# The output projection of a hybrid attention step by seven block products per group of tokens, with the sums of weight blocks kept in DRAM

## The chip, the cores and the metric

One core of one Trainium2 chip runs the kernel. The metric is device microseconds for one execution; the figure for a kernel is the median of its runs.

## The reference

One layer of an encoder. 1024 new frames of a prompt and 8 x 16 new frames of running streams (the "sample") are normalised and projected with one weight matrix into queries, keys, values and gates of two groups of eight heads: stick-breaking attention and retention. Each head's output is normalised and gated, and all are put beside each other as `y`. The part that this case is about comes last:

```python
def merge(o_sb, o_r, gate_sb, gate_r, g_sb, g_r, w_out):
    y_sb = head_rms_norm(o_sb, g_sb, gate_sb.dtype) * jax.nn.silu(gate_sb)
    y_r = head_rms_norm(o_r, g_r, gate_r.dtype) * jax.nn.silu(gate_r)
    y = jnp.concatenate([y_sb, y_r], axis=-1)
    return jnp.einsum('bte,ed->btd', y, w_out)      # y: 1024 + 128 rows of 2048; w_out: 2048 x 2048
...
xp = xp + rms_norm(out, norm_post[l])               # rms_norm(x, g) = x * rsqrt(mean(x*x) + EPS) * g
xs = xs + rms_norm(out, norm_post[l])
```

Everything is float32.

## The kernel before

Tokens come in tiles of 128 rows: eight of the prompt (0 to 7) and the sample tile. They form two groups: tiles 0 to 3 with the sample, and tiles 4 to 7. For each group in turn the kernel projects head by head with weights streamed from DRAM (`project`, `project_rows`, L248 and L268) and weaves the attention and retention of the head before into it. What a head gives goes to DRAM as `s_y[group][head]`, with 128 features on the partitions and the tokens along the row.

Matrix products are made from halves. `split` (L135) takes a float32 tile and makes a rounded high part on ScalarE (L136) and the rest as a low part on VectorE (L137); three matmuls (high x high, high x low, low x high) give the product. A weight tile is loaded by the SP queue into `wr`, then split into `wh` and `wl`; the pool `wp` has four buffers of each.

The order of the woven work is set by a clock of ticks. The code that emits matmuls calls `tick()` (L180) after every few of them; a `Job` is a generator that yields after how many ticks it wants its next step, and each tick runs one step of one job that is due. `drain(job)` ticks without matmuls until a job is done. Each engine and each queue runs its instructions in the order in which they were emitted.

The output projection (`out_panel`, L1048, and `out_project`, L1101) takes the nine tiles in three chunks of three. For a chunk it runs over four panels of 512 columns of `w_out`, and in each over 16 blocks of 128 rows: one weight tile is loaded and split and used by three tiles, nine matmuls (L1066 to L1068). `load_moving` (L203) loads and splits the rows of `y` of the next chunk meanwhile, as a job. Behind each panel `take` (L1115) squares the accumulator for the norm on ScalarE (L1117) and multiplies it by the gain on VectorE (L1118); after the last panel `store` (L1125) scales, adds the residual row `xr` on VectorE (L1131) or GpSimd (L1129) and sends the row out. For the last chunk the last 256 columns of the weights are kept on chip (`keep_last`, L1090), so that each tile can be finished by itself at the end (L1173 to L1175).

In the second group of tokens GpSimd has the masks of attention (L511) and issues the transfers that turn the attention rows through DRAM (L479, L486).

Of the kernel before, what the change touches and what calls it, by code (L numbers as in the profile page):

```python
# [9 lines left out]
F32 = mybir.dt.float32  # L10
# [6 lines left out]
P = 128  # L17
D = 2048
# [32 lines left out]
D_KL = 29  # L51
# [5 lines left out]
D_TK = 4  # L57
D_FIN = 4
D_MR = 6
EPS = 1e-6  # L60
# [5 lines left out]
def tile_hybrid_step(  # L66
# [62 lines left out]
    s_S = [scr.tile([P, P], F32, name=f"s_S{h}") for h in range(H)]  # L129
    s_y = [  # L130
# [72 lines left out]
    def load_moving(mov, at, n, src, stage=None):  # L203
        hi, lo = mov
        for k in range(KT):
            q, j = divmod(k, WQ)
            if q == len(hi):
                for x, y in zip(mov, moving_part(mp, NMAX, q)):
                    x.append(y)
            pool, bufs = stage or (wp, 2)  # L210
            r = pool.tile([P, n], F32, name="mr", tag="mr", bufs=bufs)
            nc.sync.dma_start(r, src(k))
            split(hi[q][:, j, at : at + n], lo[q][:, j, at : at + n], r)
            yield D_MR

# [38 lines left out]
    def project_pair(g, mov, cols, loads=None):  # L254
# [3 lines left out]
        for w in range(KT // WQ):  # L258
            for i, (acc, chunk) in enumerate(zip(accs, chunks)):
                _, wh, wl = next(chunk)  # L260
                for _ in range(WQ if loads and w and i == 0 else 0):
                    next(loads)
# [5 lines left out]
    def project_rows(g, mov, col, dst, off, loads=None):  # L268
# [5 lines left out]
        for w in range(KT // 2):  # L274
# [5 lines left out]
            for _ in range(WQ if loads and w == 0 else 0):  # L280
                next(loads)
# [25 lines left out]
    with ExitStack() as s1:  # L307
# [621 lines left out]
        from_y = lambda k: s_y[0][k][:, : 3 * P]  # L929
        ret_job = sb_job = sub = loads = after = None  # L930
        for gi, g in enumerate(GROUPS):
# [7 lines left out]
            for h in range(H):  # L939
# [28 lines left out]
                def attention():  # L968
# [4 lines left out]
                    if gi == 1 and h == 0:  # L973
# [3 lines left out]
                        ip = s1.enter_context(tc.tile_pool(name="ip2", bufs=1))  # L977
                    q2 = [kq.tile([P, NB_TOK], F32R, name=f"q{c}", tag=f"q{c}") for c in "hl"]
# [31 lines left out]
                def gates():  # L1010
# [6 lines left out]
                    loads = load_moving(after, 0, *((NB_TOK, from_h), (3 * P, from_y, (ip, 6)))[gi])  # L1017
# [19 lines left out]
        main = after  # L1037

        def part(gi, tiles, mov, at):
            return [(t, gi, mov, at + i * P) for i, t in enumerate(tiles)]  # L1040

        def fetch(chunk):
            _, gi, mov, at = chunk[0]
            n = len(chunk) * P
            lo = GROUPS[gi]["tiles"].index(chunk[0][0]) * P
            yield from load_moving(mov, at, n, lambda k: s_y[gi][k][:, lo : lo + n])

        def out_panel(chunk, p, pools, ticks, loads=None, between=None, width=512):  # L1048
            pool = pools[p % len(pools)]
            cols = slice(p * 512, p * 512 + width)  # L1050
            acc = [pool.tile([P, 512], F32, name="a3", tag=f"acc{n % 2}") for n in range(len(chunk))]
            for k in range(KT):
                if loads and k < WQ:
                    next(loads)
                wr = wp.tile([P, width], F32, name="wr3", tag="wr")
                load = nc.sync.dma_start(wr, w_out[0, k * P : (k + 1) * P, cols])
                if between and k % 6 == 5:
                    with tc.issue_after(load.ins):
                        next(between, None)
                wh = wp.tile([P, width], F32R, name="wh3", tag="wh")  # L1060
                wl = wp.tile([P, width], F32R, name="wl3", tag="wl")
                split(wh, wl, wr)
                q, j = divmod(k, WQ)
                for a, (_, _, (hi, lo), at) in zip(acc, chunk):
                    ts = slice(at, at + P)
                    nc.tensor.matmul(a[:, :width], hi[q][:, j, ts], wh, start=(k == 0), stop=False)  # L1066
                    nc.tensor.matmul(a[:, :width], hi[q][:, j, ts], wl, start=False, stop=False)  # L1067
                    nc.tensor.matmul(a[:, :width], lo[q][:, j, ts], wh, start=False, stop=(k == KT - 1))  # L1068
                    for _ in range(ticks):
                        tick()  # L1070
            return acc

        chunk1 = part(0, (0, 1, 2), main, 0)
        panel0 = out_panel(chunk1, 0, (accp,), D_OUT, loads)
# [3 lines left out]
    with ExitStack() as s3:  # L1078
        c3 = s3.enter_context(tc.tile_pool(name="c3", bufs=1))
        rp = s3.enter_context(tc.tile_pool(name="rp", bufs=1))  # L1080
        accq = s3.enter_context(tc.tile_pool(name="accq", bufs=2, space=PSUM))
# [6 lines left out]
        LAST = slice(7 * 256, 8 * 256)  # L1088

        def keep_last(at):  # L1090

            hi, lo = main
            for q in range(KT // WQ):
                for j in range(0, WQ, 2):
                    wr = wp.tile([P, 2, 256], F32, name="wr4", tag="wr")
                    k = (q * WQ + j) * P
                    nc.sync.dma_start(wr, w_out[0, k : k + 2 * P, LAST].rearrange("(k p) e -> p k e", p=P))
                    split(hi[q][:, j : j + 2, at : at + 256], lo[q][:, j : j + 2, at : at + 256], wr)
                    yield D_KL

        def out_project(chunk, panel0=None, kept=None):  # L1101
            m = len(chunk)
            parts = 4 if kept is None else 5
            outs = [rp.tile([P, D], F32, name="out", tag="out", bufs=5) for _ in chunk]
            ssq = rp.tile([P, m, 5], F32, name="ssq3", tag="ssq3", bufs=2)
            xrs = []

            def load_x_rows():
                for t, _, _, _ in chunk:
                    xr = rp.tile([P, D], F32, name="xr", tag="xr", bufs=3)  # L1110
# [157 lines left out]
```

## Time and profile before

| | |
|---|---|
| runs | 2385.1, 2389.83, 2397.73 us; median 2389.83 |
| profiled execution | 2393.5 us, of which the span of instructions is 2391.8 us |
| TensorE busy in the span | 2320.5 us (97%) |
| VectorE, ScalarE, GpSimd busy | 1255.6, 920.0 and 644.1 us |
| granted TensorE clock | 0.991 of full |
| moved by transfers | 418.68 MB, mean 175 GB/s |

Busy time counts the instructions of an engine; those that only issue a transfer or wait are left out on the other engines, while GpSimd's own transfers count as its work. A row of a group reads: line, engine, operation, out<-in, shapes, count | busy us, mean ns of one | idle us just before them, and what ended that idle time. In a row of the timeline stand the start, the length and the instruction. PE is TensorE, DVE VectorE, ACT ScalarE, POOL GpSimd, SP the queue that issues most loads.

### The profile page before, as it was taken

Reading aid. Unit: us, or ns where it says so; the run is one execution under the profiler, and the core shown is the slowest. Engines: PE = TensorE matmul, PEld = TensorE weight load, DVE = VectorE, ACT = ScalarE, POOL = GpSimd, SP = SyncE. Lnnn points to the kernel's source line nnn. Section 1 sums busy time; section 2 is a strip of 40 time slices with the busy share of each in tenths; the row PEclk is TensorE's granted clock in tenths of the full one; section 3 lists DMA queues with packets and bytes.
Section 4 is the critical chain, followed back from the end, with each engine's and each line's share of the span. In section 5 each row is a group of like instructions: output and inputs, shape, how many; then the busy total and the mean of one; then the engine's idle time right before and its main releaser. Section 6 shows DMA issues by size and latency. Waiting matters only on the chain.

```text
span 2391.8 us, 40520 instructions
## 1 busy us (share of the span) xinstructions
PE 2320.5 (97%) x14832; PEld 2092.4 (87%) x14832; DVE 1255.6 (52%) x2442; ACT 920.0 (38%) x1937; POOL 644.1 (27%) x1033
## 2 busy tenths in 40 slices
PE   7999999999999999999899999999999999999998
PEld 7998899998999999998778989889898888888887
DVE  7245545455545555456545554554554566564544
ACT  6323333333333333334333334333343444443443
POOL 3144354434445353434202112020220220000000
PEclk9999999999999999999999999999999999999999
DMA  7659779796989979698866565555655666765563
GB/s 245 163 131 215 161 162 200 163 200 153 199 177 200 188 163 205 158 207 221 187 182 154 139 149 154 139 145 151 150 154 134 161 160 197 229 211 182 188 192 131
DMA packets 677049, 418.68 MB, mean 175 GB/s; under 512 B 224752, under 2 KB 620016, under 8 KB 674544
## 3 DMA queue, kind: packets, MB, share of 16 engines
q1 hardware_dynamic: 524272, 285.99, 48.0%
q0 software_dynamic: 32256, 71.36, 13.9%
q10 hardware_dynamic: 120320, 58.74, 9.1%
q8 instruction: 116, 1.90, 0.4%
q14 instruction: 85, 0.70, 0.1%
HBM read 336.24 MB, written 79.69 MB: 174 GB/s over the span
## 4 chain that ended last, share of the span: by engine, by line
PE 71%; DMA 6%; DVE 4%; issue 2%; ACT 2%; SPq 1%; POOL 0%; DVEq 0%; ACTq 0%; POOLq 0%
PE acc L234 36%; PE accn L293 12%; PE a L1067 5%; PE a L1066 5%; PE a L1068 5%; PE pa L623 2%; PE z L593 2%; DMA wr<-w_in 2%; PE zc L672 1%; PE pd L741 1%; DMA mr<-s_y 1%; DMA mr<-s_h 1%; DMA dT<-c_dt 1%; DVE wl L137 1%; PE pa L786 1%
## 5 line engine op out<-in xcount | busy, mean ns | idle before, releaser
L234 PE MATMUL acc<-mh,wh 128*128 128x256 f32 (+2 forms) x2304 | 667.2, 341 | 7.8 <-ACT wh L136 7.2
L137 DVE TENSOR_TENSOR wl<-wr,wh 128x512 fp32r<-128x512 f32 (+1 forms) x576 | 391.4, 684 | 517.7 <-ACT wh L136 500.8
L234 PE MATMUL acc<-ml,wh 128*128 128x256 f32 (+2 forms) x2304 | 661.5, 339 | 0.0
L234 PE MATMUL acc<-mh,wl 128*128 128x256 f32 (+2 forms) x2304 | 660.8, 339 | 0.0
L136 ACT ACTIVATE wh<-wr 128x512 fp32r<-128x512 f32 (+1 forms) x576 | 358.0, 625 | 726.6 <-PE acc L234 229.7
L234 PEld LDWEIGHTS acc<-mh,wh 128*128 128x128 f32 x2304 | 421.2, 189 | 40.5 <-ACT wh L136 9.0
L234 PEld LDWEIGHTS acc<-mh,wl 128*128 128x128 f32 x2304 | 424.5, 189 | 31.7 <-issue 2.5
L234 PEld LDWEIGHTS acc<-ml,wh 128*128 128x128 f32 x2304 | 425.5, 189 | 28.6 <-issue 0.8
L656 POOL DMA_DIRECT2D kc<-cache_sb_k x512 | 332.5, 655 | 344.4 <-DVE kcT L696 209.5
L293 PE MATMUL accn<-whn,mh 128*128 128x256 f32 x1152 | 329.2, 287 | 4.6 <-DVE rg L320 4.5
L293 PE MATMUL accn<-wln,mh 128*128 128x256 f32 x1152 | 326.3, 284 | 2.4 <-DVE wln L137 2.4
L293 PE MATMUL accn<-whn,ml 128*128 128x256 f32 x1152 | 325.9, 284 | 0.0
L293 PEld LDWEIGHTS accn<-whn,mh 128*128 128x128 f32 x1152 | 220.9, 192 | 8.5 <-DVE rg L320 4.8
L293 PEld LDWEIGHTS accn<-wln,mh 128*128 128x128 f32 x1152 | 221.7, 192 | 3.4 <-DVE wln L137 2.6
L293 PEld LDWEIGHTS accn<-whn,ml 128*128 128x128 f32 x1152 | 221.3, 192 | 0.0
L1067 PE MATMUL a<-wl,mh 128*128 128x512 f32 (+1 forms) x576 | 219.4, 381 | 1.1 <-DVE wl L137 1.1
L1066 PE MATMUL a<-wh,mh 128*128 128x512 f32 (+1 forms) x576 | 218.9, 381 | 0.1
L1068 PE MATMUL a<-wh,ml 128*128 128x512 f32 (+1 forms) x576 | 218.9, 380 | 0.0
L137 DVE TENSOR_TENSOR wln<-wrn,whn 128x512 fp32r<-128x512 f32 x128 | 87.3, 689 | 125.1 <-ACT whn L136 124.8
L136 ACT ACTIVATE whn<-wrn 128x512 fp32r<-128x512 f32 x128 | 79.6, 632 | 164.7 <-PE acc L234 70.7
L486 POOL DMA_DIRECT2D be<-s_be x128 | 94.3, 743 | 132.4 <-DMA s_be<-be 114.5
L1067 PEld LDWEIGHTS a<-wl,mh 128*128 128x128 f32 x576 | 108.3, 188 | 22.4 <-DVE wl L137 2.2
(195 smaller groups left out, 2617.6 us busy)
## 6 DMA issues: line engine op xcount, KB each, us to landing
wr<-w_in SPq DMA_DIRECT2D x384, 256.0 KB, 4.2
wr<-w_out SPq DMA_DIRECT2D x184, 256.0 KB, 3.6
wrn<-w_in SPq DMA_DIRECT2D x128, 256.0 KB, 3.3
kc<-cache_sb_k POOLq DMA_DIRECT2D x512, 64.0 KB, 4.7
vc<-cache_sb_v SPq DMA_DIRECT2D x64, 512.0 KB, 9.0
xt<-x_prompt SPq DMA_DIRECT2D x8, 1024.0 KB, 6.0
xr<-x_prompt SPq DMA_DIRECT2D x8, 1024.0 KB, 6.2
out<-out ACTq DMA_DIRECT2D x24, 256.0 KB, 3.4
```

The costliest lines, as they stand in the source:

```text
L136: nc.scalar.activation(hi, src, AF.Copy)
L137: nc.vector.tensor_tensor(lo, src, hi.bitcast(F32), ALU.subtract)
L234: last = nc.tensor.matmul(a[:, :m], lhs[:, j, :], rhs[w][:, j, o : o + m], start=(w == 0 and j == 0 and n == 0), stop=(w == KT // WQ - 1 a ...
L293: anchor[0] = nc.tensor.matmul(a, lhs[q][:, jj, ts], rhs[:, j, :], start=(w == 0 and j == 0 and n == 0 and t % 2 == 0), stop=(w == KT // 2 ...
L486: q.dma_start(raw[32 * i : 32 * i + 32, :].rearrange("p (k a) -> p k a", a=32), s[:, :, 32 * i : 32 * i + 32].rearrange("k (j b) a -> b (k ...
L593: nc.tensor.matmul(z[:, :c], q2[a][:, i * P : (i + 1) * P], k2[b][:, s : s + c], start=(m == 0), stop=(m == 2),)
L623: nc.tensor.matmul(po[:, :P], at[:, j, :], vn[:, j, :], start=(j == 0), stop=(j == t))
L656: nc.gpsimd.dma_start(kc[32 * i : 32 * i + 32, :].rearrange("p (k d) -> p k d", d=32), cache_k[0, 2 * c + j, s * 512 : (s + 1) * 512, h, 3 ...
L672: mm = nc.tensor.matmul(z[r, :], qp[:, j, r], ready[2 * j + c // 2][:, c % 2, :], start=(j == 0), stop=(j == 1),)
L1066: nc.tensor.matmul(a[:, :width], hi[q][:, j, ts], wh, start=(k == 0), stop=False)
L1067: nc.tensor.matmul(a[:, :width], hi[q][:, j, ts], wl, start=False, stop=False)
L1068: nc.tensor.matmul(a[:, :width], lo[q][:, j, ts], wh, start=False, stop=(k == KT - 1))
```

## The change

The rows of four token tiles are halved into two pairs of tiles (`th`), the 2048 features into two halves (`kk`), the columns of `w_out` into two halves. In place of the eight products of halves there are seven, each of a sum or difference of two halves of `y` (or one half alone) with a sum or difference of two blocks of `w_out` (or one block alone). Each product is added to or subtracted from one or two quarters of the result. The table `SEVEN` lists for each product the halves of `y` and their sign, the weights (a number is a sum kept in DRAM, a pair a block of `w_out` itself) and the quarters that receive it. The sample tile has only its four plain products with unsummed blocks; they ride on the products whose weights are plain (2 to 5, table `ALSO`).

- `weight_sums` makes the five sums of weight blocks: a job that starts in the second token group, loads pieces of `w_out` on SP, adds on GpSimd and stores to `s_b` in DRAM from GpSimd's queue.
- `operand` loads the halves of `y` for one product from `s_y`, adds them on GpSimd, and splits the sum; it runs as a job during the product before.
- `product` runs over two panels of 512 columns with eight weight blocks each; a block now serves two tiles (six matmuls) or three with the sample.
- `collect` and `gather`, a job after each panel, bring the accumulators into rows on chip: ScalarE copies the first contribution, VectorE adds the later ones. `complete` squares a finished piece on ScalarE and multiplies it by the gain on GpSimd; `finish` stores a tile when its four pieces are done.
- At the end the last five weight blocks are kept on chip and used tile by tile.

`load_moving`, `project_pair` and `project_rows` change only in small ways (no `stage` argument; a load that has run out is not an error). The removed functions are those of the output projection that are printed above.

```diff
-D_TK = 4
-D_FIN = 4
+D_TK = 2
+D_FIN = 3
+D_OP = 3
+D_SB = (30, 6, 14)
+HT = KT // 2
+HALF = D // 2
+SEVEN = (
+    (((0, 0), (1, 1)), 1, 0, ((0, 0, 1), (1, 1, 1))),
+    (((1, 0), (1, 1)), -1, 4, ((0, 0, 1),)),
+    (((0, 0), (1, 0)), 1, (1, 1), ((0, 0, -1), (0, 1, 1))),
+    (((1, 1),), 1, 2, ((0, 0, 1), (1, 0, 1))),
+    (((0, 0),), 1, 1, ((0, 1, 1), (1, 1, 1))),
+    (((0, 1), (1, 1)), 1, (0, 0), ((1, 0, 1), (1, 1, -1))),
+    (((0, 1), (0, 0)), -1, 3, ((1, 1, 1),)),
+)
+ALSO = {2: ((0, 1), 1), 3: ((1,), 0), 4: ((0,), 1), 5: ((0, 1), 0)}
+KEPT = 5
...
+    def weight_sums(pool):
+        for k in range(HT):
+            for c in range(4):
+                cs = slice(c * 256, (c + 1) * 256)
+                r = pool.tile([P, 2, 2, 256], F32, name="br", tag="br", bufs=2)
+                for kk in range(2):
+                    rows = w_out[0, (kk * HT + k) * P : (kk * HT + k + 1) * P, :]
+                    nc.sync.dma_start(r[:, kk], rows.rearrange("p (a n) -> p a n", a=2)[:, :, cs])
+                yield D_SB[0]
+                o = pool.tile([P, 5, 256], F32, name="bo", tag="bo", bufs=1)
+                for j, (x, y, f) in enumerate(((0, 3, ALU.add), (1, 3, ALU.subtract), (2, 0, ALU.subtract))):
+                    a, b = (r[:, z // 2, z % 2, :] for z in (x, y))
+                    nc.gpsimd.tensor_tensor(o[:, j, :], a, b, f)
+                    yield D_SB[1]
+                nc.gpsimd.tensor_tensor(o[:, 3:5, :], r[:, :, 0, :], r[:, :, 1, :], ALU.add)
+                nc.gpsimd.dma_start(s_b[c // 2][k][:, :, (c % 2) * 256 : (c % 2 + 1) * 256], o)
+                yield D_SB[2]
+
+    def operand(gi, n, bufs, pool=None, deep=2):
...
+        def load(h):
+            r = bufs.tile([P, 2, 256], F32, name="yr", tag="yr", bufs=deep + 2)
+            for i, (kk, th) in enumerate(terms):
+                nc.sync.dma_start(r[:, i], s_y[gi][kk * H + h][:, th * 256 : (th + 1) * 256])
...
+        def add(r, several, how):
+            if several:
+                nc.gpsimd.tensor_tensor(r[:, 0], r[:, 0], r[:, 1], how)
+            return r[:, 0]
...
+        for h in range(HT):
+            if h + deep < HT:
+                load(h + deep)
+            r, rs = loaded.pop(0)
+            split(mov[0][:, h], mov[1][:, h], add(r, len(terms) > 1, ALU.add if sign > 0 else ALU.subtract))
+            if also:
+                split(mov[2][:, h], mov[3][:, h], add(rs, len(also) > 1, ALU.add))
+            yield D_OP
...
+                        sums.append(Job(weight_sums(ip), D_SB[0]))
...
-                    loads = load_moving(after, 0, *((NB_TOK, from_h), (3 * P, from_y, (ip, 6)))[gi])
+                    loads = operand(0, 0, ip, None, 1) if gi else load_moving(after, 0, NB_TOK, from_h)
...
+        for _ in loads:
+            pass
+        drain(sums[0])
...
+        def times(a, x, k, ts, wh, wl, first, last):
+            hi, lo = x
+            nc.tensor.matmul(a, hi[:, k, ts], wh, start=first, stop=False)
+            nc.tensor.matmul(a, hi[:, k, ts], wl, start=False, stop=False)
+            nc.tensor.matmul(a, lo[:, k, ts], wh, start=False, stop=last)
...
+        def product(gi, n, nh, ticks, upto=HT):
+            mov, kind = ops[gi, n], SEVEN[n][2]
+            todo = [(accp.tile([P, 512], F32, name="a3", tag=f"acc{p}"), mov[:2], TS[p]) for p in range(2)]
+            if len(mov) > 2:
+                todo.append((accq[0].tile([P, 512], F32, name="as", tag="accs"), mov[2:], TS[0]))
+            for k in range(upto):
+                wh, wl = load_split(kind, nh, k)
+                for a, x, ts in todo:
+                    times(a, x, k, ts, wh, wl, k == 0, k == HT - 1)
                     for _ in range(ticks):
                         tick()
...
+        def collect(gi, n, nh, accs):
+            for p in range(2):
+                for th, half, sign in SEVEN[n][3]:
+                    gather((gi, 2 * th + p), half, nh, accs[p], sign)
+                    yield D_TK
+            if len(accs) > 2:
+                gather((0, 4), ALSO[n][1], nh, accs[2], 1)
+                yield D_TK
...
+            if piece not in begun:
+                begun.add(piece)
+                left[piece] = 2 if key[1] == 4 else TERMS[key[1] // 2, half]
+                nc.scalar.activation(o, a, AF.Copy)
+            else:
+                nc.vector.tensor_tensor(o, o, a, ALU.add if sign > 0 else ALU.subtract)
+            left[piece] -= 1
+            if not left[piece]:
+                complete(key, 2 * half + nh, o, cols)
...
+        def complete(key, c, o, cols):
+            square(key, c, o)
+            nc.gpsimd.tensor_tensor(o, o, gpost[:, cols], ALU.mult)
+            if len(ssqs[key][1]) == 4:
+                finishing[key] = Job(finish(key), D_FIN)
...
+        Job(collect(0, 1, 1, product(0, 1, 1, 1)), D_TK)
+        seq = [(0, n) for n in range(2, 7)] + [(1, n) for n in range(7)]
+        nxt = Job(operand(0, 2, rp, ss), D_OP)
+        last = seq[-1]
+        for i, (gi, n) in enumerate(seq):
+            drain(nxt)
...
+                nxt = Job(operand(g2, n2, rp, None if g2 or n2 == 6 else ss), D_OP)
...
+            for nh in range(2):
+                if (gi, n, nh) == (*last, 1):
+                    break
+                accs = product(gi, n, nh, 1)
...
+                Job(collect(gi, n, nh, accs), D_TK)
...
+        accs = product(1, 6, 1, 1, HT - KEPT)
+        for k in range(KEPT):
+            wr = wp.tile([P, 512], F32, name="wr3", tag="wr")
+            nc.sync.dma_start(wr, weights_of(kind, 1, HT - KEPT + k))
+            split(kh[:, k], kl[:, k], wr)
+        while jobs:
+            tick()
+        rows = [load_rows((1, 2 + p)) for p in range(2)]
+        cols = slice(3 * 512, D)
+        for p in range(2):
+            key = 1, 2 + p
+            for k in range(KEPT):
+                k1 = HT - KEPT + k
+                times(accs[p], ops[1, 6][:2], k1, TS[p], kh[:, k], kl[:, k], False, k1 == HT - 1)
+            o = outs[key][:, cols]
+            nc.vector.tensor_tensor(o, o, accs[p], ALU.add)
+            square(key, 3, o)
...
```

More of the change, by code (lines that the diff above doesn't have):

```diff
@@ L1036, in tile_hybrid_step @@
                     ret_values(g, mov, h + 1)
[L1037 to L1068, printed above, removed]
@@ L1086, in tile_hybrid_step @@
             )
[L1088 to L1099, printed above, removed]
```

210 lines of the change are left out of this document (113 added, 97 removed).

## The prediction

> **What bounds the kernel now.** I read the page first, then busy time by stretches, single TensorE instructions, groups by shape, and last the waits. The page:
>
> ```profile
> PE 2320.5 (97%) x14832; PEld 2092.4 (87%) x14832; DVE 1255.6 (52%) x2442; ACT 920.0 (38%) x1937; POOL 644.1 (27%) x1033
> ```
>
> 97% is a mean. By stretches (first token group, second token group, output projection, tail):
>
> ```profile
> core 0: us, PE busy (x) PEld busy (x) DVE busy (x) ACT busy (x) POOL busy (x), PEclk, DMA share, GB/s
> 120.00:1180.00 1060.00, 1030.45 (x7695) 970.56 (x7693) 548.53 (x1146) 365.10 (x797) 453.10 (x753) 0.99 0.84 182
> 1260.00:1940.00 680.00, 674.31 (x3806) 589.50 (x3805) 362.64 (x627) 266.71 (x554) 123.27 (x192) 1.00 0.58 147
> 1982.00:2382.00 400.00, 398.54 (x1904) 335.02 (x1902) 207.53 (x373) 171.81 (x364) 15.32 (x11) 1.00 0.60 189
> 2020.00:2100.00 80.00, 80.00 (x355) 66.24 (x354) 42.85 (x84) 39.16 (x93) 0.00 (x0) 1.00 0.70 224
> ```
>
> The projection runs 400 us with TensorE idle for 1.5 us, at the full clock, while VectorE is half busy. Fewer products shorten it only while the other engines keep up. A recorded matmul overlaps the next one, so the price is the step from start to start:
>
> ```profile
> 2339.77 0.39 PE L1067 MATMUL a<-wl,mh 128*128 128x512 f32 x1
> ...
> 2346.80 0.39 PE L1068 MATMUL a<-wh,ml 128*128 128x512 f32 x1
> 2347.03 0.28 PE L1066 MATMUL a<-wh,mh 128*128 128x256 f32 x1
> ...
> 2357.10 0.28 PE L1066 MATMUL a<-wh,mh 128*128 128x256 f32 x1
> ```
>
> From 2339.77 to 2347.03 there are 32 steps: 0.227 us for 512 columns. From there to 2357.10 there are 84: 0.12 us for 256 columns. The groups by shape give the counts (L1066 and L1068 have the same count as L1067; L1174 and L1175 as L1173):
>
> ```profile
> L1067 PE MATMUL a<-wl,mh 128*128 128x512 f32 x528 | 205.8, 390 | 1.1 <-DVE wl L137 1.1
> L1173 PE MATMUL a<-mh 128*128 128x256 f32 x48 | 13.6, 283 | 0.0
> L1067 PE MATMUL a<-wl,mh 128*128 128x256 f32 x48 | 13.6, 283 | 0.0
> ```
>
> 3 x 528 x 0.227 + 6 x 48 x 0.12 = 359.6 + 34.6 = 394 of the 400 us. TensorE's own rate is the bound.
>
> **What is removed.** By the code the new stage has 2 groups x 7 products x 2 column panels x 8 blocks x 2 tiles x 3 = 1344 matmuls of 512 columns, and 192 for the sample tile: 1536 x 0.227 = 348.7 us. Gain: 394 - 349 = **45 us**. What replaces the rest decides.
>
> **Weights are now shared by fewer rows.** A block of weights used to serve three tiles (9 matmuls, 2.04 us). It serves two in 160 of the 224 blocks (6 matmuls, 1.36 us), three in the 64 with the sample. In the second group of products 112 blocks take 112 x 1.36 = 152 us of TensorE. Against that, from these rows:
>
> ```profile
> L137 DVE TENSOR_TENSOR wl<-wr,wh 128x512 fp32r<-128x512 f32 x225 | 154.6, 695 | 166.4 <-ACT wh L136 157.3 <-DMA mr<-s_y 2.4 <-PE pa L623 2.2
> L136 ACT ACTIVATE wh<-wr 128x512 fp32r<-128x512 f32 x225 | 140.2, 629 | 200.1 <-PE a L1068 112.2 <-PE acc L234 39.6 <-DMA wr<-w_out 13.0
> L1118 DVE TENSOR_TENSOR out<-a,gpost 128x512 f32<-128x512 f32 x33 | 22.7, 689 | 3.3 <-ACT wh L136 2.0 <-ACT sq L1117 0.5
> L1117 ACT ACTIVATE sq<-a 128x512 f32<-128x512 f32 x33 | 19.6, 593 | 0.9 <-PE a L1068 0.3
> L1117 ACT ACTIVATION_READ_ACCUMULATOR sq<-a 128x1 f32 x39 | 7.6, 194 | 0.0
> ```
>
> and from the timeline, two operations back to back:
>
> ```profile
> 2067.16 0.63 DVE L137 TENSOR_TENSOR ml<-mr,mh 128x256 fp32r<-128x256 f32 x2 [2.39 <-ACT mh L136]
> 2067.89 1.30 DVE L137 TENSOR_TENSOR wl<-wr,wh 128x512 fp32r<-128x512 f32 x2
> ```
>
> VectorE back to back: 112 weight splits at 0.65 (half of 1.30), 56 operand splits at 0.315, 32 gathers out of the accumulators at 0.69 (nearest row L1118, also from an accumulator), 8 stores at 0.74 (row below): 73 + 18 + 22 + 6 = 119 of 152 us. It fits, but beside GpSimd it may not:
>
> ```profile
> L399 POOL TENSOR_TENSOR xt<-xt,gpre x24: 727/737/1244, 13.6 to 33.3; 128x256 f32<-128x256 f32 x24
> L1129 POOL TENSOR_TENSOR out<-out,xr x11: 1276/1415/1776, 2121.9 to 2385.1; 128x512 f32<-128x512 f32 x11
> ```
>
> ```profile
> 2125.39 0.74 DVE L1131 SCALAR_TENSOR_TENSOR out<-out,out3r,xr 128x512 f32<-128x512 f32 x1
> 2128.58 1.80 DVE L1131 SCALAR_TENSOR_TENSOR out<-out,out3r,xr 128x512 f32<-128x512 f32 x1
> 2128.54 1.29 POOL L1129 TENSOR_TENSOR out<-out,xr 128x512 f32<-128x512 f32 x1 [4.95 <-ACT out L1128]
> ```
>
> The VectorE operation that began just behind a GpSimd one took 1.80 us where it takes 0.74: it waited out the other. The second group gets 40 operand sums (0.74), 16 multiplications by the gain and 8 additions (1.28): 60 us of GpSimd. VectorE operations with two on-chip inputs are 97 of the 152 us; if that share (63%) of the 60 us falls on VectorE, it needs 119 + 38 = 157, so **+4 us** (0 if none, 119 + 60 - 152 = 27 if all). The Trainium skill, page SBUF — State Buffer, section "SBUF: two separate sides", speaks against moving sums to GpSimd: a VectorE operation with two inputs in that memory and a GpSimd operation exclude each other for their whole length. The trace agrees, with its 1.80 against 0.74 us; by the rule alone the floor would be 97 + 60 = 157 us.
>
> **Boundaries of products: +27 and +9.** The gather waits for the product's last matmul, and it is issued when only block 0 of the next product has been split. Behind it in VectorE's and ScalarE's queues stand all later weight splits. Where a gather completes a piece, the row's square follows on ScalarE. From the end of the product: 0.16 (0.39 less the step 0.227) + gather 0.69 + square 0.59 + 0.19 + split 0.63 + 0.69 = 2.95 us until block 1 is whole; TensorE needs it after 1.36 + 0.23 = 1.59. Stall 1.36 us; with the sample 0.68. Pieces: 14 in the second group, 4 in product 6 of the first, 16 beside the sample: 24.5 + 10.9 = 35 us. Operand steps (10 in 32 ticks) push about a third of the first gathers behind the next split, where they cost nothing; I take three quarters, 27 (0 to 35). Where the operand is not done in 32 ticks, draining it puts the gather even before block 0: 0.16 + 0.69 + 0.63 + 0.69 = 2.2 us at 8 boundaries; half of them, 9 (0 to 18).
>
> **The loop of the four weight buffers: +12.**
>
> ```profile
> wr<-w_out SPq DMA_DIRECT2D x184, 256.0 KB, 3.6
> wr<-w_in SPq DMA_DIRECT2D x384, 256.0 KB, 4.2
> wr<-w_in SPq DMA_DIRECT2D x144, 256.0 KB, 6.4
> ```
>
> ```profile
> L1056 SPq DMA_DIRECT2D wr<-w_out x192: 327/328/1762, 1957.0 to 2356.9; - x192
> ```
>
> ```profile
> SPq L1056 <- DVE wl L137: 163.4, 130, 3.9
> ```
>
> (The 6.4 is from 300 to 1100 us, where transfers crowd.) SP already waits 163 us for the split that frees a buffer. A turn is issue 0.33 + landing 3.6 + 0.63 + 0.69 = 5.25, a quarter of it 1.31 us per block: under the 2.04 of now, a hair under the 1.36 of later. With 0.8 us of queueing on both engines it is 1.51, 0.15 x 160 = 24 us, half of which I put inside the boundary stalls: 12. Ends: 0, and with landing 4.2 and 1.0 of queueing 1.71, 56 us.
>
> **Smaller terms: +10.** The sums in the second group add 96 x 0.74 + 32 x 1.28 = 112 us to GpSimd, and 32 stores:
>
> ```profile
> L479 POOL DMA_DIRECT2D s_be<-be x28 | 25.4, 906 | 150.7 <-DVE be L523 149.0 <-DVE ro L795 1.7
> ```
>
> at 0.9 that is 29 more, and 38 MB of transfers (16.8 MB of weights read, five quarters of that written). In GpSimd's queue, attention's masks and its turned rows stand behind them; VectorE waits for those, and weight splits stand behind VectorE. TensorE's lead of some blocks at 12 x 0.227 = 2.7 us hides that. Its idle share is 0.8% here (680 - 674.3) and 2.8% in the first group, where GpSimd and transfers are as busy as this stage will be: 0 to 13 us, I take 4, nearer to this stage's own row. Hand-over: a GpSimd sum of 0.74 now stands ahead of the first operand splits, +3 (0 to 8). Tail: the last five weight blocks come at 1.3 us each while the first tile uses them at 0.68, +3 (0 to 5); after the last matmul the same operations follow as now.
>
> Sum: -45 + 4 + 27 + 9 + 12 + 10 = **+17 us**. The profiled execution took 2393.5 us (span 2391.8), 3.7 above the median 2389.8 of the runs; so 2410 by the profile, **2406** by the median. About 0.5% (12 us) is what a measurement of this kernel can tell from no change.
>
> **Rivals.**
> 1. TensorE stays the bound and keeps the gain: splits run far enough ahead, since ScalarE and VectorE idle half of the time now and delayed gathers slip behind block 1. For it: the last panel used a 128 KB block per 9 x 0.12 = 1.08 us without idling. Place: block 1 after each boundary; it decides if that block is whole within 1.59 us. Then only the 10 us and some two stay: 2390 - 45 + 12 = 2357. Chance 0.34.
> 2. The stalls are half of mine for boundaries and loop (24 instead of 48): 2406 - 24 = 2382; with the spread between them, within 12 us of no change. Chance 0.15.
> 3. Transfers decide. The second group moves 112 x 0.262 (weights) + 96 x 0.131 (operands) + 8.4 (inputs and outputs of four tiles) = 50 MB in 152 us, 331 GB/s; the row 2020:2100 has 224 GB/s at share 0.70, which scales to 320 at 1. If landing goes to 6.4, a block takes (0.33 + 6.4 + 0.63 + 0.69) / 4 = 2.01 us: 160 x 0.65 = 104; 2390 - 45 + 104 + 10 = 2459. Against it: packets of 2 KB here, smaller there. Chance 0.18.
> 4. All 60 us of GpSimd fall on VectorE, 27 in place of 4: 2406 + 23 = 2429. For it the 1.80 us row, against it that VectorE often waits anyway. Chance 0.06.
>
> **How the numbers follow.** The forecast itself has 0.27. Faster by over 0.5%: rival 1, 0.34. Within: rival 2, 0.15. Slower: 0.27 + 0.18 + 0.06 = 0.51. The likeliest side's own range is 2402 to 2459. The whole range reaches from just under rival 1 to just under rival 3: 2354 to 2456.
>
> **What would show it.** Right: 1536 matmuls of 512 columns in the stage; TensorE idle 40 to 70 us there, in pieces of 1 to 2 us behind each product, released by VectorE's or ScalarE's weight splits; VectorE over 75% busy in the second group of products, with operations of 1.3 us and more beside GpSimd's. The second token group stays within 10 us of its length. Rival 1 shows as TensorE at 99% in the stage, rival 3 as ScalarE waiting for landings of 5 us and more. Wrong would be a stage shorter than 375 us, or idle time that grows in the second token group by over 15 us.

## The result and the profile after

The changed kernel takes 2489.56 us (median of 4 runs, 2482.62 to 2492.68) against 2387.47 us for the kernel before, run beside it: **1.0416 times, interval 1.0376 to 1.0457**. Forecast were 2406 us and a range up to 2456. The sign was right (slower had been given a chance of 0.51), the size was not: the profiled span grew by 99.2 us (2391.8 to 2491.0), not by 17.

The page of the changed kernel, engines first:

```profile
PE 2325.8 (93%) x14496; PEld 2065.2 (83%) x14496; DVE 1387.3 (56%) x2584; ACT 973.9 (39%) x2062; POOL 933.0 (37%) x1328
```

TensorE has 336 recorded matmuls fewer, and its share falls from 97% to 93%: the time went into waiting. Busy time by stretches of the changed kernel (first token group; three pieces of the second; the projection to the end) says where:

```profile
120.00:1180.00 1060.00, 1029.91 (x7684) 970.94 (x7682) 547.95 (x1145) 364.69 (x797) 451.39 (x752) 0.99 0.84 182
1260.00:1400.00 140.00, 122.87 (x622) 106.02 (x623) 75.41 (x106) 44.79 (x95) 87.26 (x104) 0.91 0.90 242
1400.00:1600.00 200.00, 175.39 (x944) 151.59 (x943) 102.70 (x170) 65.39 (x142) 101.68 (x122) 0.94 0.81 213
1600.00:1800.00 200.00, 198.30 (x1142) 174.29 (x1141) 106.21 (x181) 77.31 (x159) 36.65 (x56) 1.00 0.59 147
2041.00:2491.00 450.00, 387.40 (x1568) 293.68 (x1566) 319.58 (x536) 232.53 (x499) 151.09 (x142) 0.95 0.74 235
```

The columns are those of the same view before. The first token group is unchanged (1029.91 of 1060 us). In the second, TensorE loses 17 us of 140 and 25 of 200, with GpSimd more than half busy and the granted clock at 0.91 to 0.94; from 1600 on it is at 99% again. The first weight load of the projection, of before and then of the changed kernel:

```profile
L1066 PEld LDWEIGHTS a<-wh,mh x576: 186/188/192, 1982.0 to 2363.8; 128*128 128x128 f32 x192
```

```profile
L1122 PEld LDWEIGHTS a<-wh,mh x438: 186/188/334, 2041.0 to 2467.9; 128*128 128x128 f32 x146
```

So **59.0 us were lost before the projection began** (2041.0 less 1982.0), and the projection to the end of the span took 450.0 us instead of 409.8, **40.2 us more**. Together 99.2.

**The second token group.** GpSimd's groups, the waits and a stretch of GpSimd's timeline, all of the changed kernel, 1180 to 1640 us for the first two:

```profile
L242 POOL TENSOR_TENSOR bo<-br 128x256 f32<-128x256 f32 x96 | 81.8, 877 | 137.8 <-DMA s_b<-bo 79.4 <-PE acc L306 48.3 <-DMA br<-w_out 10.0
L244 POOL TENSOR_TENSOR bo<-br 128x512 f32<-128x512 f32 x32 | 43.5, 1359 | 0.0
```

```profile
POOL bo L242 <- DMA s_b<-bo: 79.4, 24, 6.1
...
DVE kp L594 <- POOL kp L583: 47.4, 10, 13.6
...
PEld pa L695 <- DVE kp L655: 27.0, 6, 8.8
```

```profile
1303.73 3.96 POOL L242 TENSOR_TENSOR bo<-br 128x256 f32<-128x256 f32 x3 [2.19 <-DMA s_b<-bo]
1307.66 1.28 POOL L244 TENSOR_TENSOR bo<-br 128x512 f32<-128x512 f32 x1
1309.35 0.83 POOL L245 DMA_DIRECT2D s_b<-bo  x1 [0.41 <-POOL bo L244]
1310.04 2.42 POOL L558 DMA_DIRECT2D be<-s_be  x3
```

All 96 + 32 additions lie in this one stretch (the rounds from 1224 to 1567 us), though the group runs to 2041. A round is three short additions, a long one and a store; there is one `bo` buffer, so the next round waits until the store has landed (24 waits, 79.4 us). Attention's turned rows (`be`, L558) and masks (L583) stand behind such rounds in GpSimd's queue. VectorE then waits up to 13.6 us for a mask, TensorE up to 8.8 us for `kp`. The chain that ends in TensorE's longest wait of the stretch, from the timelines of three engines:

```profile
1501.06 2.07 POOL L242 TENSOR_TENSOR bo<-br 128x256 f32<-128x256 f32 x3 [6.15 <-DMA s_b<-bo]
1503.09 0.28 POOL L583 TENSOR_SCALAR_AFFINE_SELECT kp<-kp 128x128 f32<-128x128 f32 x1
...
1503.40 1.56 DVE L594 TENSOR_TENSOR_SCAN kp<-kp 128x640 f32<-128x640 f32 x1 [13.57 <-POOL kp L583]
1504.89 1.68 DVE L152 TENSOR_TENSOR wln<-wrn,whn 128x512 fp32r<-128x512 f32 x1
...
1506.62 0.29 PEld L365 LDWEIGHTS accn<-wln,mh 128*128 128x128 f32 x1 [9.47 <-DVE wln L152]
```

The mask stands behind a round that waited for its store; VectorE's scan waits 13.57 us for the mask, a weight split (`wln`) stands behind the scan, and TensorE waits 9.47 us for the split. SyncE's queue is held up as well, which is easily overlooked:

```profile
SPq L237 <- POOL bo L244: 87.3, 20, 11.1
...
ACT wh L151 <- DMA wr<-w_in: 63.0, 18, 15.3
```

```profile
1493.69 13.55 SPq L237 DMA_DIRECT2D br<-w_out  x4
```

The loads of pieces for the sums (`br`, L237) wait there until GpSimd frees a buffer, and loads of weights stand behind them: ScalarE waits 63.0 us for weights in this stretch, against 5.3 in the kernel before. TensorE's own waits there are 27.0 us for `kp` and 20.0 for `wln`; each of the three waits for `wln` ends just behind a late mask.

**The projection.** The recorded matmuls are the 1536 of 512 columns that were counted (438 + 64 + 10 in each of three lines), and they follow each other at 0.227 us as before wherever TensorE hasn't just waited (the last section has the exception); but weights come late. VectorE's weight split and TensorE's waits, from 2041 us:

```profile
L152 DVE TENSOR_TENSOR wl<-wr,wh 128x512 fp32r<-128x512 f32 x216 | 176.1, 824 | 103.4 <-ACT wh L151 98.9 <-DMA yr<-s_y 1.4 <-DMA ys<-s_y 1.4
```

```profile
PEld a L1123 <- DVE wl L152: 39.1, 56, 2.9
PEld a L1122 <- ACT wh L151: 34.9, 22, 7.3
```

The split into `wl` takes 0.824 us where it took 0.695. The two waits and four small groups make 83.4 us, against 2.9 us before. They are waits of weight loads, and part of each passes while the matmul before still runs. Worked out from the starts of the matmuls in the trace, waiting lengthens the steps by about 58 us, and about 18 us more are 113 matmuls that ran slower (over 0.41 us) behind waits. At the end, the changed kernel's timeline:

```profile
2476.79 0.39 PE L1124 MATMUL a<-mh,ml 128*128 128x512 f32 x1
...
2478.54 1.75 DVE L1297 SCALAR_TENSOR_TENSOR og<-og,outr,xr 128x512 f32<-128x512 f32 x1
...
2480.22 0.68 DVE L1290 TENSOR_TENSOR out<-out,a 128x512 f32<-128x512 f32 x1
```

The last tile's accumulator is full at 2477.2 but is read at 2480.2: VectorE still scales the tile before it for its store. From the last matmul to the end of the span it is 13.8 us; before it was 10.0 (last matmul 2381.5 + 0.28). The stage then adds up: 1536 x 0.227 = 348.7, waits 58, slower matmuls 18, tail 13.8, and some 12 us of small delays and late matmuls of attention, 450.

### The profile page after: what moved, and what is told of

It is laid out like the page before. It is cut to its first block, busy times and chain, and to the rows that moved or that the text cites. A ratio compares the mean times of both kernels' runs of the same rounds, so it can differ in the third digit from the quotient of the medians.

```text
span 2491.0 us, 40888 instructions
## 1 busy us (share of the span) xinstructions
PE 2325.8 (93%) x14496; PEld 2065.2 (83%) x14496; DVE 1387.3 (56%) x2584; ACT 973.9 (39%) x2062; POOL 933.0 (37%) x1328
## 4 chain that ended last, share of the span: by engine, by line
PE 22%; DMA 11%; POOL 6%; DVE 6%; issue 5%; ACT 2%; SPq 0%; DVEq 0%; ACTq 0%; POOLq 0%
PE acc L306 11%; PE accn L365 4%; POOL bo L242 3%; DMA wr<-s_b 3%; DMA s_b<-bo 3%; DVE wl L152 2%; POOL bo L244 1%; PE pa L695 1%; DMA yr<-s_y 1%; PE a L1123 1%; POOL be L558 1%; PE a L1122 1%; DMA wr<-w_out 1%; PE a L1124 1%; ACT wh L151 1%
## 5 line engine op out<-in xcount | busy, mean ns | idle before, releaser
L152 DVE TENSOR_TENSOR wl<-wr,wh 128x512 fp32r<-128x512 f32 x603 | 452.2, 756 | 472.8 <-ACT wh L151 455.5
L151 ACT ACTIVATE wh<-wr 128x512 fp32r<-128x512 f32 x603 | 377.4, 630 | 725.0 <-PE acc L306 244.2
L1122 PE MATMUL a<-wh,mh 128*128 128x512 f32 x438 | 175.5, 406 | 27.5 <-ACT wh L151 25.2
L1123 PE MATMUL a<-wl,mh 128*128 128x512 f32 x438 | 181.0, 413 | 18.1 <-DVE wl L152 17.2
L1124 PE MATMUL a<-wh,ml 128*128 128x512 f32 x438 | 175.4, 401 | 0.6 <-DVE ml L152 0.6
L151 ACT ACTIVATE whn<-wrn 128x512 fp32r<-128x512 f32 x128 | 79.4, 633 | 170.8 <-PE acc L306 63.8
L558 POOL DMA_DIRECT2D be<-s_be x128 | 95.2, 776 | 103.0 <-DMA s_be<-be 72.1
L242 POOL TENSOR_TENSOR bo<-br 128x256 f32<-128x256 f32 x96 | 81.8, 877 | 137.8 <-DMA s_b<-bo 79.4
```

The source lines that it names most:

```text
L151: nc.scalar.activation(hi, src, AF.Copy)
L152: nc.vector.tensor_tensor(lo, src, hi.bitcast(F32), ALU.subtract)
L242: nc.gpsimd.tensor_tensor(o[:, j, :], a, b, f)
L558: q.dma_start(raw[32 * i : 32 * i + 32, :].rearrange("p (k a) -> p k a", a=32), s[:, :, 32 * i : 32 * i + 32].rearrange("k (j b) a -> b (k ...
L1122: nc.tensor.matmul(a, hi[:, k, ts], wh, start=first, stop=False)
L1123: nc.tensor.matmul(a, hi[:, k, ts], wl, start=False, stop=False)
```

## The experiments

Four causes stood against each other. **Q**: the sums' place in GpSimd's queue delays attention. **B**: at each boundary of products the gathers delay the next splits, as forecast. **P**: VectorE and GpSimd block each other. **W**: four weight buffers are too short a loop. "Stalls" are TensorE's weight-load waits in the projection, 83.4 us in the change; they serve to compare the runs.

**The sums alone, in the kernel before** (sums_alone: `weight_sums` is added to it, nothing reads them, and its projection stays).

```diff
+                        sums.append(Job(weight_sums(ip), D_SB[0]))
...
-                    loads = load_moving(after, 0, *((NB_TOK, from_h), (3 * P, from_y, (ip, 6)))[gi])
+                    loads = load_moving(after, 0, *((NB_TOK, from_h), (3 * P, from_y, (ip, 4)))[gi])
...
+        drain(sums[0])
```

> The old kernel with only the weight sums added in the second token group (loads, GpSimd sums, stores to DRAM); nothing reads them, and the first operand loads of the projection have four buffers in place of six. Theory Q (the sums stand in GpSimd's queue in one stretch, each waits for the store of the one before, and attention's masks and turned rows wait behind them): TensorE idles some 50 to 60 us between 1180 and 1650 us, the kernel takes about 2445. Rival: the second token group grew because of loads that the new projection brings forward (operand rows, first product), not because of the sums: 2388 to 2400.

Measured: 2451.71 us against 2386.38, ratio 1.0262 (1.0222 to 1.0302): the sums alone cost 65 us. The same stretch in the kernel before and in this one:

```profile
1180.00:1640.00 460.00, 450.10 (x2571) 390.15 (x2572) 239.90 (x445) 176.28 (x372) 72.17 (x112) 0.99 0.61 154
```

```profile
1180.00:1640.00 460.00, 409.48 (x2258) 352.29 (x2257) 228.90 (x374) 151.41 (x318) 216.67 (x259) 0.94 0.82 217
```

In the same 460 us TensorE gets through 2258 matmuls instead of 2571. The first matmul of the projection comes at 2045.6.

**The change without the sums** (no_sums: the products read plain blocks of `w_out` where the sums would stand).

```diff
-                        sums.append(Job(weight_sums(ip), D_SB[0]))
-        drain(sums[0])
...
-                return s_b[nh][k][:, kind, :]
+                kind = kind % 2, kind // 2 % 2
```

> The changed kernel without the weight sums: the five products that use a sum take a plain weight block of the same size in its place, so its output differs there. Theory Q: the second token group is back to its old length, first projection matmul near 1982, total about 2430: the projection stage alone stays some 40 us longer than the old one. Rival (the sums disturb the projection stage as well, for example through stores that land late): the stage shrinks too, under 2415.

Measured: 2442.07 us, ratio 1.0224 (1.0191 to 1.0256). The first matmul of the projection comes at 1985.6, stalls are 86.5 us. The second token group is whole again, and the projection is as bad as in the change: two separate losses.

**The sums tied to the matmuls** (sums_tied: the whole work; each load and addition of the sums is held, for the order of the queues alone, behind the matmul that was last emitted).

```diff
+    def follow(ins):
+        tc.add_manual_dep(
+            ins.ins,
+            anchor[0].ins.name,
+            mybir.DependencyInfo(mybir.DependencyClass.NoSync, mybir.DependencyReason.SCHED_ONLY),
+            reason="tied to the products",
+        )
...
-                    nc.sync.dma_start(r[:, kk], rows.rearrange("p (a n) -> p a n", a=2)[:, :, cs])
+                    follow(nc.sync.dma_start(r[:, kk], rows.rearrange("p (a n) -> p a n", a=2)[:, :, cs]))
...
-                    nc.gpsimd.tensor_tensor(o[:, j, :], a, b, f)
+                    follow(nc.gpsimd.tensor_tensor(o[:, j, :], a, b, f))
```

> The changed kernel with each load and each sum of the weight sums tied, in the order of its queue, behind the matmul at which its job emits it; same work, same bytes, spread over the second token group in place of one stretch at its start. Theory Q: most of the 60 us come back, 2432 to 2445. Rival P (VectorE is held by GpSimd's sums) and rival T (38 MB more of transfers slow the weight loads): work and bytes are the same, so little comes back, 2470 to 2490.

Measured: 2432.9 us, ratio 1.0196 (1.0157 to 1.0236); the first matmul of the projection comes at 1986.4.

```profile
1180.00:1640.00 460.00, 446.32 (x2550) 386.20 (x2549) 269.51 (x434) 174.23 (x365) 184.16 (x225) 0.99 0.78 208
```

The same additions, loads and stores, spread over more of the group: 2550 matmuls in the stretch, and 57 us less than the change. Q is shown: not the work of the sums but where it stands cost some 55 of the 59 us (first matmul 2041.2 in the change). The edit ties the loads on SyncE's queue and the additions on GpSimd's at once. The waits above lead over GpSimd's queue to TensorE; what SyncE's queue added to it was not run by itself. ScalarE's wait for weights in the stretch falls from 63.0 to 11.3 us.

**A free buffer for the first operand of the second group, and an earlier start of operand (0,2)** (operand_free). The trigger was the longest stall: SyncE's timeline of the changed kernel, and TensorE's just after.

```profile
2094.48 0.32 SPq L1130 DMA_DIRECT2D wr<-s_b  x1
2094.85 0.90 SPq L262 DMA_DIRECT2D ys<-s_y  x2
2095.79 0.90 SPq L257 DMA_DIRECT2D yr<-s_y  x2
...
2104.38 0.85 SPq L262 DMA_DIRECT2D ys<-s_y  x2
2105.28 0.43 SPq L1130 DMA_DIRECT2D wr<-w_out  x1
```

```profile
2109.51 0.29 PEld L1122 LDWEIGHTS a<-wh,mh 128*128 128x128 f32 x1 [7.32 <-ACT wh L151]
```

Between two loads of weights SyncE issued operand loads for 10.4 us; at 2109.5 TensorE had waited 7.32 us.

```diff
-            mov.append(mp.tile([P, HT, 256], F32R, name=f"m{s}{n % 2}", tag=f"m{s}{n % 2}"))
+            mov.append(mp.tile([P, HT, 256], F32R, name=f"m{s}{(n + gi) % 2}", tag=f"m{s}{(n + gi) % 2}"))
...
+        nxt = Job(operand(0, 2, rp, ss), D_OP)
         Job(collect(0, 1, 1, product(0, 1, 1, 1)), D_TK)
...
-        nxt = Job(operand(0, 2, rp, ss), D_OP)
```

> The changed kernel with two operand preparations freed: product 0 of the second group writes its operand into the other buffer than product 6 of the first group still reads, and the operand of product 2 starts one product earlier. Weight sums as in the change. Theory O (part of the projection's stalls is operands that are not ready: 7.3 us before product 2, about 15 us at the start of the second group): the stage is 15 to 20 us shorter, 2470. Rival B (stalls are the short ones at each product's start and the weight buffers): nothing, 2486 to 2492.

Measured: 2484.79 us, ratio 1.0404 (1.036 to 1.0449), stalls 77.5. Less than 5 us against the change, below what can be told apart: these single long stalls were not the main matter.

**Both repairs together** (tied_free), the base of all that follows.

> Weight sums tied to the matmuls and the two operands freed, together; the base of the three runs beside it. From the runs so far 2433 less about 5 to 8: 2425 to 2430, still some 40 us above the kernel before, with the projection stage idle on TensorE for about 72 us.

Measured: 2428.44 us (the kernel before beside it: 2392.68), ratio 1.0141 (1.0117 to 1.0164). TensorE's waits and VectorE's split, 1985 to 2400 us:

```profile
PEld a L1131 <- DVE wl L152: 44.6, 58, 2.7
PEld a L1130 <- ACT wh L151: 33.9, 24, 5.0
```

```profile
L152 DVE TENSOR_TENSOR wl<-wr,wh 128x512 fp32r<-128x512 f32 x214 | 177.3, 837 | 95.1 <-ACT wh L151 90.9 <-DMA ys<-s_y 2.7
```

**Boundaries: the first gather of each product eight ticks later** (late_gather).

```diff
-                Job(collect(gi, n, nh, accs), D_TK)
+                Job(collect(gi, n, nh, accs), 8)
```

> tied_free with the first gather of a product's accumulators given 8 ticks in place of 2 behind its last matmul, so that about four weight blocks of the next product are split ahead of it. Theory B (stalls sit at the starts of products, where gather and square stand in front of the next weight splits): 20 to 27 us less, about 2402. Rivals P (VectorE held by GpSimd) and W (four weight buffers): no change, within 6 us of tied_free.

Measured: 2425.9 us, ratio 1.0125 (1.0093 to 1.0157), stalls 73.4. The intervals overlap: where the gathers stand decides little. B falls as the main cause.

**Port: no GpSimd arithmetic in the projection's stream** (no_gp: the sums of operands and the multiplications by the gain are left out; operands and rows are then other data).

```diff
-                nc.gpsimd.tensor_tensor(r[:, 0], r[:, 0], r[:, 1], how)
-            nc.gpsimd.tensor_tensor(o, o, gpost[:, cols], ALU.mult)
```

> tied_free with GpSimd's operand sums and gain multiplications of the projection left out (the product uses the first half of y alone, finished pieces stay without the gain), so only the additions of the stores remain on GpSimd there. Theory P (VectorE's operations with two on-chip inputs wait while a GpSimd operation runs, and operand splits wait for sums): VectorE's weight split goes from a mean of 0.82 back to about 0.70 us and 25 us or more come back, 2400 or less. Rivals B and W: under 8 us, since operand and gain work is not on their path.

Measured: 2409.08 us, ratio 1.0056 (1.0035 to 1.0078): 19.4 us less than tied_free.

```profile
L152 DVE TENSOR_TENSOR wl<-wr,wh 128x512 fp32r<-128x512 f32 x216 | 153.7, 719 | 112.8 <-ACT wh L151 109.0 <-DMA ys<-s_y 2.7 <-issue 0.2
```

```profile
PEld a L1130 <- ACT wh L151: 25.6, 16, 6.9
PEld a L1131 <- DVE wl L152: 23.7, 37, 2.6
```

VectorE's split goes from 0.837 to 0.719 us though VectorE itself does the same work. The run also takes GpSimd out of the operands' chain (add, then split), so not all of the 19 us need be the blocking itself.

**Weight loop: eight raw weight buffers in the projection instead of four** (deep_w; the whole work, the split parts keep four; the eight serve from the second panel of product 1 on).

```diff
-            wr = wp.tile([P, 512], F32, name="wr3", tag="wr")
+            wr = wpool[-1].tile([P, 512], F32, name="wr3", tag="wr")
...
+        wpool.append(s3.enter_context(tc.tile_pool(name="dw", bufs=8)))
```

> tied_free with eight buffers for the loaded weight blocks of the projection in place of four (the split halves keep four). Theory W (a turn of four buffers, issue, landing and two splits, takes longer than four blocks of products): 12 to 25 us less, 2402 to 2415. Rivals B and P: within 5 us of tied_free.

Measured: 2407.94 us (10 runs), ratio 1.0069 (1.004 to 1.0097): 20.5 us less than tied_free. ScalarE's wait for weights from `s_b` falls from 46.6 us (first row, tied_free) to 9.2; TensorE's waits of deep_w follow.

```profile
ACT wh L151 <- DMA wr<-s_b: 46.6, 31, 4.8
```

```profile
ACT wh L151 <- DMA wr<-s_b: 9.2, 6, 3.5
```

```profile
PEld a L1131 <- DVE wl L152: 33.5, 36, 2.5
PEld a L1130 <- ACT wh L151: 19.3, 13, 3.9
```

**Port and loop together** (deep_nogp: both edits; the same parts are left out as in no_gp).

> As deep_w (sums tied to matmuls, operands freed, eight buffers for the raw weight tiles of the projection), with the operand sums and the gain multiplications on GpSimd left out (operands and rows are then other data; all copies, loads and matmuls stay). Theory that port and weight loop are two separate causes: their gains against tied_free (19 us and 20 us) add up, the stalls in the stage fall from 54.9 us to below 36 and the time to 2386 to 2393, ratio 1.000 or below. Rival, that both take the same slack (either one gives VectorE its lead back): they do not add up, stalls stay at 45 to 55 us and the time is 2402 to 2408.

Measured: 2389.17 us (10 runs) against 2390.07, ratio 0.9993 (0.9976 to 1.001).

```profile
PEld a L1130 <- ACT wh L151: 17.2, 11, 4.2
PEld a L1131 <- DVE wl L152: 11.4, 16, 2.5
```

19.4 + 20.5 were expected if the causes are separate, 39.3 were found. The kernel before ran 2.6 us faster beside this run than beside tied_free; by the ratios, 0.0085 + 0.0072 were expected and 0.0148 found. Either way P and W add up, and stalls fall to 30 us. What is left includes whatever the boundaries cost.

**Operand loads from ScalarE's queue** (deep_act, on deep_w), and **late gathers on top** (deep_act_late).

```diff
-                nc.sync.dma_start(r[:, i], s_y[gi][kk * H + h][:, th * 256 : (th + 1) * 256])
+                nc.scalar.dma_start(r[:, i], s_y[gi][kk * H + h][:, th * 256 : (th + 1) * 256])
```

> As deep_w, with the loads of the operands' tiles issued by ScalarE's queue instead of SyncE's, so that no load of weights stands behind them. If what is left of the weight loop is the order of loads on SyncE's queue: stalls fall from 54.9 us by 8 to 15 and the time to 2393 to 2400. Rival, VectorE's copies are the limit late in the stage: stalls stay within 5 us of 54.9 and the time within 5 us of 2408. Rival, the issuing takes ScalarE's time for the splits: ScalarE's wh stalls grow above 25 us and the time goes above 2411.

> As deep_act, with the first gather of each product eight ticks later (late_gather on top). Boundary theory: below 3 us against deep_act, as it gave 2.5 us alone. This is the best version that the runs point to; expected 2390 to 2402, ratio 1.000 to 1.006 against the kernel before: no faster than it.

Measured: 2433.43 us, ratio 1.0179 (1.0164 to 1.0194), and 2428.23 us, ratio 1.0162 (1.0136 to 1.0188). A miss, 25 us worse than deep_w. TensorE's waits of deep_act, up to its end:

```profile
PEld a L1130 <- ACT wh L151: 36.4, 16, 5.0
PEld a L1131 <- DVE wl L152: 31.0, 39, 3.1
```

The stall on ScalarE's `wh` rose from 19.3 to 36.4 us while that on VectorE stayed about as it was (33.5 and 31.0): the second rival's sign. The issues delay ScalarE's splits here. Whether it is the time of the issues (about 0.33 us each) or the waits that stand in the queue ahead of them (up to 3.3 us) was not separated. On top of it late_gather gave some 5 us, with intervals that overlap.

**Operand sums on VectorE** (deep_dve, on deep_w).

```diff
-                nc.gpsimd.tensor_tensor(r[:, 0], r[:, 0], r[:, 1], how)
+                nc.vector.tensor_tensor(r[:, 0], r[:, 0], r[:, 1], how)
```

> As deep_w, with the sums of the operands' tiles (about 96 additions, 0.96 us each on GpSimd) made by VectorE instead; the gain multiplications stay on GpSimd. All of the computation is done. If GpSimd's holding of the shared port is what costs the 19 us, VectorE's wl falls from 0.83 us to about 0.73 (216 times, 22 us back) while it takes on 80 additions of about 0.36 us and 16 of 0.25, 33 us: VectorE ends about even (314 us busy becomes 315 to 330), ScalarE waits less for the operands, and the time is 2396 to 2412, ratio 1.002 to 1.009. Rival, that the in-order place of the additions in VectorE's queue holds up the weights' second parts (an addition waits for its load, and wl stands behind it): stalls on DVE wl grow above 40 us and the time goes above 2415.

Measured: 2411.09 us, ratio 1.0091 (1.0058 to 1.0124), as expected and no better than deep_w.

```profile
L152 DVE TENSOR_TENSOR wl<-wr,wh 128x512 fp32r<-128x512 f32 x215 | 160.4, 754 | 53.3 <-ACT wh L151 52.7
...
L275 DVE TENSOR_TENSOR yr<-yr 128x256 f32<-128x256 f32 x71 | 36.5, 522 | 25.0 <-DMA yr<-s_y 25.0
```

The splits get 0.07 us back (0.825 to 0.754 us, 215 times, 15 us), and the additions take 36.5. The best version that does the whole work is deep_w, still 0.7% slower than the kernel before.

## Why the prediction was wrong, point by point

**The gain of 45 us** holds. All 1536 matmuls are there, at the old rate where TensorE hadn't waited, and deep_nogp, with 30 us of stalls, is level with the kernel before. The sum of the stage closes with 348.7 us.

**"Smaller terms", the sums in the second token group: +4 (0 to 13). This is the step that failed**, by 55 us: measured 59 in the change and 65 in sums_alone. The work was counted nearly right (112 us of additions; the trace has 125); the error was to let "TensorE's lead of some blocks" (2.7 us) hide it, without asking where it stands in the queues: single waits of TensorE reached 9.5 us. I had also written, in the section on the kernel before, that each engine runs its instructions in the order in which they were emitted. The traces show otherwise. The code asks for 62 ticks per piece (30 + 3 x 6 + 14), 1984 for all 32. In sums_tied, where each piece is held to its place, the rounds run from 1239 to 1824 us, and 24 pairs of masks lie between the first and the last; in the change they run from 1224 to 1567 us with 12 pairs between. Both emit the same instructions, so the order of a queue isn't that of the source, and what nothing holds back can move ahead. The kernel before shows it in its own code: `tied` (L158) holds instructions of the first token group to matmuls; the sums had no such tie. With it, in sums_tied, the projection's first matmul comes at 1986.4, against 1985.6 with no sums at all: the same work then costs too little to tell, since the profiles of the later runs with tied sums begin anywhere from 1978.4 to 1991.4. The price was one for an order that the change didn't have.

**VectorE beside GpSimd: +4 (0 to 27).** Mis-sized, if within its range. It asked whether 119 us of VectorE work and its share of GpSimd's fit into 152 us. No engine was full: VectorE was busy 149 of 200 us from 2240 to 2440. But the split takes longer on the mean, and TensorE then waits for it. no_gp measured 19.4 us, with the operands' chain in it; the share of the blocking alone was not separated. The Trainium skill, page SBUF — State Buffer, section "SBUF: two separate sides", calls the shared port pair an exclusive lock between a VectorE operation with two inputs there and a GpSimd operation; the traces agree in kind (0.837 against 0.719 us for the same split, and on the other side GpSimd's three additions in 3.96 us at 1303.73).

**The loop of the four weight buffers: +12 (0 to 56).** deep_w measured 20.5 us, inside the range; the turn of 5.25 us was no bad estimate, since landings stayed at 3.8 us. Rival 3, transfers at 6.4 us, did not come about.

**Boundaries: +27 and +9.** Oversized. The prediction put 27 us at the second weight block behind each boundary and 9 at the first. Worked out from the starts of the matmuls in the change's trace, about 5 of the 58 us of waiting lie at the second block of a panel and 16 at the first (7 of these are the one wait at 2109.5); the other 36 lie at the third to the eighth block, where these two terms put nothing. late_gather moved 2.5 us, and with P and W gone all stalls together are 30 us, with the boundaries unchanged. The working let every boundary cost its full delay, which the traces don't show. The same count for deep_nogp has 8 us at the first and 5 at the second block, of 24.

**Hand-over and tail, +3 each.** Without any sums the projection still begins 3.4 us later than before (1985.6 against 1982.2 for the first matmul), about the hand-over's +3, but single profiles scatter by more (above) and nothing tested its cause. The tail measured 3.8, but for another reason than the one given: the operations after the last matmul are not the same as before, since VectorE's work for the stores of the tile before stands ahead of the last gather.

So the stalls of the stage were forecast at 52 us and were 83, and the second token group at 4 and was 59. Rival 1 (2357) fails on the weights' arrival, rival 2 (half the stalls) errs to the other side; rival 4 named a cost of the right size (23 us more for the port) at a chance of 0.06.

What stays open beside this: no_sums, with fewer transfers and no sums, was not faster than sums_tied (intervals 1.0191 to 1.0256 and 1.0157 to 1.0236 overlap), and no run was made for it. In the profiles the difference lies in the projection, with 86.5 us of stalls against 78.2.

## What to carry to other kernels

Side work for an idle engine costs by where it stands in the queues, that of its engine and that of its loads: before calling it hidden, find out what holds it back from being moved ahead of the work that others wait for, and tie it to the main stream if nothing does. When a change cuts the reuse of each loaded block (here from nine matmuls to six), ask again whether the chain of load and two splits still keeps ahead with its buffers; here neither VectorE nor ScalarE was full, and still more buffers and an undisturbed VectorE were each worth about 20 us. Seven products instead of eight bought 45 us; the three side costs (queue order 55, port with the operands' chain 19, buffers 20) came to twice that.

## What was not expected of the hardware

The granted clock fell with TensorE's idle gaps: 0.91 to 0.94 in the stretch of the sums, where waits were up to 9.5 us long, against 0.99 from 1180 to 1640 us before. In the projection the slowest matmul took 0.796 us where the median is 0.389:

```profile
L1122 PE MATMUL a<-wh,mh x438: 387/389/796, 2041.2 to 2468.1; 128*128 128x512 f32 x146
```

It is the first behind the wait of 7.32 us at 2109.5, and those that follow start 0.43 us apart, where 0.227 is the rule:

```profile
2111.26 0.63 PE L1122 MATMUL a<-wh,mh 128*128 128x512 f32 x1
2111.69 0.63 PE L1123 MATMUL a<-wl,mh 128*128 128x512 f32 x1
```

This lasts until about 2114, some 4 us. So an idle gap costs more than its length: by the count above, 58 us of waiting brought 18 us of slower matmuls with it. The Trainium skill, page TensorE: Matmul & The Clock Gate, section "Part 1: The HAM clock gate", states half rate after an idle window of about 3.4 us. The steps of 0.43 and 0.227 us agree with about half. Here shorter gaps did it too: behind waits of TensorE of 2.54 us (ending at 2294.2) and 2.87 us (ending at 2298.9), matmuls again start 0.43 us apart at 2300.3 to 2301.2.
